# Half of q as a seventeenth pair of seven products, fourth block sums in place behind the last q part, and rates spread over six slots

## The chip, the cores and the metric

The kernel runs on one core of a Trainium2 chip. Its engines are TensorE (PE, with its weight loads shown as PEld), VectorE (DVE), ScalarE (ACT), GpSimd (POOL) and SyncE (SP, which issues nearly all DMAs). The metric is the device time of one execution in microseconds (us); several executions are taken and their median counts.

## The reference

One layer of a bidirectional hybrid encoder on x (1024 positions, 1024 channels, float32): an embedding LayerNorm; one input projection; two branches; a merge; an output projection; a last LayerNorm.

```python
h = layer_norm(x, emb_ln_g, emb_ln_b)
proj = h @ w_in                      # q k v z_a u z_b (512 each), g_a g_b (1024 each)
y_a = neighbourhood_attention(q, k, v, rpb) * silu(z_a)   # 8 heads x 64, q scaled by 1/8
u = centred_depthwise_conv(u, conv_w, conv_b)
y_b = (rg_lru(u, forward) + rg_lru(u, reverse)) * silu(z_b)
m = sigmoid(g_a + b0) * (y_a @ w_ba) + sigmoid(g_b + b1) * (y_b @ w_bb)
out = layer_norm(ALPHA * h + m @ w_out, ln_g, ln_b)
```

In `rg_lru`, log_a = -8 * softplus(-lambda) * r: softplus(-lambda), one number for each channel and direction, is what this text calls the rates.

## The kernel before

**Matrix products.** Every operand is split into a high and a low part of reduced width, and a product is three matmuls: high by high, low by high, high by low (`mm3`). TensorE reads 128x128 weights against 512 columns. The transposed input of the projection lies in four blocks of 512 x 512: B11, B12 (channels 0 to 511, positions 0 to 511 and 512 to 1023) and B21, B22 (channels 512 to 1023).

**Pairs of seven products.** Two blocks of 128 output columns of the input projection make a pair. A pair (`product`) is not computed as eight products of quarter size but as seven, in the manner of Strassen and Winograd: the left operands are the four weight quarters a11, a12, a21, a22 and their sums s1 = a21 + a22, s2 = s1 - a11, s3 = a11 - a21, s4 = a12 - s2; the right operands are B11, B21, B22 and the block sums T1 to T4. Each product is 12 matmuls, in the order a11, a12, s2, s1, s3, s4, a22 (`OPS`). Products s2, s3 and a22 go on into the PSUM bank of a11, s4 into that of s1 (`INTO`). Between them the bank is read out (`evacuate`): ScalarE copies it after a11 (u1) and after s2 (u2), and the bank of s1 after s1 (u3); VectorE then adds what each output block needs, and reads the bank of a11 once more after s3, ahead of a22.

**Slots.** Sixteen pairs make 112 slots, one for a product. In each slot the Python loop issues, in this order: the read-out of the product before, the high part of a weight of the next pair (`s_hi`), things hung into the slot with `at(slot, 0, ...)`, the product, the low part of a weight (`s_lo`), stores, one weight sum of the next pair (`s_sum`, slots 0 to 3) or the loads of the pair after that (`s_load`, slot 4), and things hung in with `at(slot, 1, ...)` (convolution, gates, scans of the second branch). The order of issue is written out by hand for all engines, and each engine works its queue in order.

**The stage before the pairs.** LayerNorm, transposes (`tile_in`), v (eight tiles, `v_part`, 24 matmuls each) and q. q has four blocks of 128 columns (m), each with two halves of 512 positions (n): eight parts (`q_part`) of 24 matmuls. ScalarE writes the high part of a q block (`q_hi`), VectorE the low part (`q_lo`), SP stores it to q_d (`q_store`), from where the attention loads it later. Between these, for the position tiles 4 to 7, the block sums are built: `t_full(i)` makes T1, T2 and T3, `t_last(i)` makes T4 with two VectorE subtractions and additions into a tile of its own, `t_hi` (ScalarE) and `t_lo` (GpSimd) split them. Parts (0, 0) and (1, 0) run within the v stage; the six others stand behind it. While they run, the weights of the first pair (u, columns 0 and 1) are loaded and split; those of the second are loaded behind the last q store. Then the rates follow in one piece, some 30 VectorE instructions of 8 columns with one Exp on ScalarE.

**Behind the pairs:** the attention with the second branch's projection as filler, the merge of the branches (`mb`), the output projection (`o`) with its LayerNorm.

Of the kernel before, what the change touches and what calls it, by code (L numbers as in the profile page):

```python
# [28 lines left out]
N_PAIR = 16  # L29
# [3 lines left out]
CONV_AT = (7, 24, 45, 66)  # L33
GATE_AT = (14, 24, 35, 45, 56, 66, 77, 87)
LATE_AT = (102, 102, 103, 104, 105)
HEAD_AT = 109
LO_POOL = ("a11", "a22")
HI_POOL = ("a12", "s2", "s1", "s3", "s4")
U_PAIRS = (0, 5)
# [28 lines left out]
def encoder_kernel(ctx, tc, x, gb1, gb, w_qk, w_v, w_s, w_ba, w_bb, w_gate, smalls, bias, w_out, out):  # L68
# [223 lines left out]
    def t_full(i):  # L292

        tt[i, 3] = wsp.tile([P, 4, P], F32, tag="a22", bufs=2, name=f"t3_{i}")[:]
        t12 = ln.tile([P, 2, 4, P], F32, tag="x", bufs=5, name=f"t12_{i}")
        tt[i, 1], tt[i, 2] = t12[:, 0], t12[:, 1]
        if i in (4, 6):
            tt["last"] = ln.tile([P, 2, 4, P], F32, tag="x", bufs=5, name=f"t4_{i}")
        tt[i, 4] = tt["last"][:, i % 2]
# [7 lines left out]
    def t_last(i):  # L307
        t4 = tt[i, 4]
        V.tensor_tensor(t4, f(B21[0], i), tt[i, 2], ALU.subtract)
        V.tensor_tensor(t4, t4, f(B21[1], i), ALU.add)  # L310
# [58 lines left out]
    def s_load(p, *names):  # L369
        for o in names if p < N_PAIR else ():  # L370
            t = wsp.tile([P, 4, P], F32, tag=o, bufs=2 if o == "a22" else 1, name=f"{o}_{p}f")
            SP.dma_start(t[:], w_s[p, ("a11", "a21", "a12", "a22").index(o)])
            s_a[p, o] = t

    def s_sum(p, *names):
        for o in names if p < N_PAIR else ():
            a, b, op = dict(s1=("a21", "a22", ALU.add), s2=("s1", "a11", ALU.subtract),
                            s3=("a11", "a21", ALU.subtract), s4=("a12", "s2", ALU.subtract))[o]
            t = s_a[p, o] = wsp.tile([P, 4, P], F32, tag=o, name=f"{o}_{p}f")
            V.tensor_tensor(t[:], s_a[p, a][:], s_a[p, b][:], op)  # L380
# [152 lines left out]
    qk_load(2)  # L533
# [10 lines left out]
    t_last(4)  # L544
    tile_in(5)
    q_hi(0, 0)
    t_hi(4, 2, 1, 3, 4)
    t_lo(4, 2, 1, 3, 4)
# [3 lines left out]
    keep(7)  # L552
    q_part(1, 0)
    t_full(5)
# [3 lines left out]
    t_last(5)  # L558
# [4 lines left out]
    t_hi(5, 2, 1, 3, 4)  # L563
    t_lo(5, 2, 1, 3, 4)
# [906 lines left out]
```

## Time and profile before

| | |
|---|---|
| three runs | 677.56, 678.9, 678.63 us; median 678.63 |
| profiled execution | 678.46 us, span 676.7 us, 9344 instructions |
| busy share of the span | PE 98%, PEld 82%, DVE 73%, ACT 54%, POOL 53% |
| granted TensorE clock, mean | 0.997 |
| chain that ended last | PE 89%, DVE 6%, DMA 2%, others about 1% or less |

The span runs from the first to the last instruction of the profiled execution; its own time is 1.8 us longer. In the rows of a timeline the first number is the start from the beginning of the span, the second the time that the instructions of the row took, and x the number of instructions; in brackets stands the idle time of that engine before the row and what ended it. A row of TensorE's waits has the total, the number of times and the longest, in us.

### The profile page before, as it was taken

The numbers are of one execution on the slowest core, as the hardware profiler recorded it, in microseconds if no ns is written. First come the engines' busy times: TensorE is split into PE (matmuls) and PEld (weight loads), VectorE is DVE, ScalarE is ACT, GpSimd is POOL, SyncE is SP. The second block draws the span as 40 slices with busy tenths as digits, with TensorE's granted clock in tenths as the row PEclk, the third lists the DMA queues.
The fourth block names the chain that finished last, engine by engine and source line by source line (L and its number), as shares of the span: only waits on it lengthen the run. The fifth ranks groups of instructions, "written<-read, shape, count | busy, mean of one in ns | idle before, by whom it ended". The sixth has DMA issues, their size and how long they took to land.

```text
span 676.7 us, 9344 instructions
## 1 busy us (share of the span) xinstructions
PE 665.2 (98%) x3201; PEld 555.7 (82%) x3201; DVE 492.7 (73%) x821; ACT 364.5 (54%) x612; POOL 355.8 (53%) x258
## 2 busy tenths in 40 slices
PE   8999999999999999999999999999999999999995
PEld 6888888888888887888788888888888878888884
DVE  6978747886998699879967785477787787443434
ACT  6554433256786676669576634477777554210110
POOL 6798632434677576567647444116155456334442
PEclk9999999999999999999999999999999999999998
DMA  8654353233434133431553456998793467412211
GB/s 326 244 179 170 122 206 126 77 110 123 125 128 144 40 103 115 170 126 48 195 178 122 173 191 254 316 366 296 255 323 132 162 220 281 178 62 94 93 63 62
DMA packets 48702, 113.39 MB, mean 168 GB/s; under 512 B 5056, under 2 KB 9744, under 8 KB 47120
## 3 DMA queue, kind: packets, MB, share of 16 engines
q1 hardware_dynamic: 48624, 112.81, 47.2%
q8 instruction: 25, 0.41, 0.3%
q14 instruction: 21, 0.17, 0.1%
q10 hardware_dynamic: 32, 0.01, 0.0%
HBM read 77.11 MB, written 35.68 MB: 167 GB/s over the span
## 4 chain that ended last, share of the span: by engine, by line
PE 89%; DVE 6%; DMA 2%; issue 1%; SPq 1%; ACT 0%; POOL 0%; DVEq 0%; POOLq 0%
PE a L134 30%; PE o L134 13%; PE mb L134 12%; PE s L134 11%; PE q L134 6%; PE v L328 6%; PE acc L1107 3%; PE s L1061 3%; PE pt L1083 3%; PE g L759 2%; DMA wqk_s<-in_w_qk_dram 2%; DVE ws_l L128 1%; PE tp L270 1%; DMA rsb<-rs_d 1%; DVE uc L717 1%
## 5 line engine op out<-in xcount | busy, mean ns | idle before, releaser
L134 PE MATMUL o<-wo_h,ml 128*128 128x512 f32 (+1 forms) x136 | 51.2, 377 | 0.0
L134 PE MATMUL o<-wo_l,mh 128*128 128x512 f32 (+1 forms) x136 | 51.2, 376 | 0.0
L134 PE MATMUL o<-wo_h,mh 128*128 128x512 f32 (+1 forms) x136 | 51.2, 376 | 0.0
L134 PE MATMUL a<-ht_h,ws_h 128*128 128x512 f32 x128 | 50.0, 390 | 0.0
L134 PE MATMUL a<-ht_l,ws_h 128*128 128x512 f32 x128 | 49.8, 389 | 0.0
L134 PE MATMUL a<-ht_h,ws_l 128*128 128x512 f32 x128 | 49.8, 389 | 0.0
L134 PE MATMUL a<-b_h,wa_h 128*128 128x512 f32 x128 | 49.8, 389 | 0.0
L134 PE MATMUL a<-b_h,wa_l 128*128 128x512 f32 x128 | 49.8, 389 | 0.0
L134 PE MATMUL a<-b_l,wa_h 128*128 128x512 f32 x128 | 49.8, 389 | 0.0
L1071 DVE CUSTOM_DVE_ANT_0 sc<-s,bias 128x384 f32<-128x384 f32 (+1 forms) x64 | 33.4, 522 | 21.6 <-PE s L1061 14.2
L1361 DVE SCALAR_TENSOR_TENSOR z<-z,o 128x512 f32<-128x512 f32 (+1 forms) x17 | 11.2, 656 | 51.0 <-PE o L134 51.0
L1091 ACT CAST pt_h<-pt 128x384 fp32r<-128x384 f32 x64 | 29.0, 453 | 25.3 <-PE pt L1083 17.3
L1371 POOL TENSOR_TENSOR z<-z,gb 128x1024 f32<-128x1024 f32 x7 | 16.8, 2400 | 48.5 <-ACT z L1370 48.5
L1076 ACT ACTIVATE p<-sc,summ 128x384 f32<-128x384 f32 (+1 forms) x64 | 37.8, 591 | 5.5 <-DVE summ L1071 5.3
L1340 ACT ACTIVATE sd<-mv,eps_z 128x1 f32<-128x1 f32 x8 | 2.4, 294 | 67.1 <-DVE mv L1366 67.1
L128 DVE TENSOR_TENSOR pt_l<-pt,pt_h 128x384 fp32r<-128x384 f32 x64 | 33.2, 519 | 2.1 <-ACT pt_h L1091 1.6
L328 PE MATMUL v<-wv,b_h 128*128 128x512 f32 x128 | 32.9, 398 | 0.6 <-ACT b_h L279 0.5
L867 POOL CAST wb_h<-wb 128x512 fp32r<-128x512 f32 x9 | 7.0, 779 | 47.4 <-DMA wb<-in_w_bb_dram 47.4
L1061 PE MATMUL s<-ks,qs 128*128 128x384 f32 (+1 forms) x128 | 31.4, 327 | 0.0
L1083 PEld LDWEIGHTS pt<-ident,p 128*128 128x128 f32 x176 | 23.1, 140 | 8.5
L1083 PE MATMUL pt<-ident,p 128*128 128x128 f32 x176 | 29.6, 272 | 0.0
L128 POOL TENSOR_TENSOR wb_l<-wb,wb_h 128x512 fp32r<-128x512 f32 x16 | 22.0, 1375 | 14.3 <-ACT wb_h L865 13.6
(438 smaller groups left out, 2204.2 us busy)
## 6 DMA issues: line engine op xcount, KB each, us to landing
ks<-k_d SPq DMA_DIRECT2D x8, 1024.0 KB, 7.5
h_d<-x SPq DMA_DIRECT2D x8, 512.0 KB, 5.0
v_d<-vs SPq DMA_DIRECT2D x8, 512.0 KB, 3.7
q_d<-q SPq DMA_DIRECT2D x8, 512.0 KB, 3.1
ga_d<-ga SPq DMA_DIRECT2D x16, 256.0 KB, 2.2
gb_d<-gb SPq DMA_DIRECT2D x16, 256.0 KB, 2.6
k_d<-k SPq DMA_DIRECT2D x8, 512.0 KB, 3.4
qs<-q_d SPq DMA_DIRECT2D x8, 512.0 KB, 5.5
```

Of the source, the lines that this page charges most:

```text
L128: eng.tensor_tensor(lo, full, hi.bitcast(F32), ALU.subtract)
L134: PE.matmul(o, a, b, start=first and i == 0, stop=last and i == len(prods) - 1, skip_group_check=not (first and last))
L328: PE.matmul(vos[i][:], a, wv[kind == "w"][k][:], start=vn[i] == 0, stop=vn[i] == 23)
L759: PE.matmul(o[:, n, :], w[:, 2 * d + b, :], us[b][:, n * HALF:(n + 1) * HALF], start=z == 0, stop=z == 1)
L1061: PE.matmul(o[:, :P * len(near(t))], q[:, t * P:(t + 1) * P], k[:, z, keys], start=z == 0, stop=z == 1)
L1071: V.tensor_tensor_reduce(s[:, :w], o[:, :w], heads[h][2][:, b0:b0 + w], -1.0, 3.0e38, ALU.add, ALU.min, accum_out=sums[h][0][:, t:t + 1])
L1076: A.activation(probs[h % 2][t][:], scs.pop((h, t))[:, :w], AF.Exp, bias=sums[h][0][:, t:t + 1], scale=-1.0, accum_out=sums[h][1][:, t:t + 1])
L1083: PE.transpose(tp[:, n * P:(n + 1) * P], probs[h % 2][t][:, z * P:(z + 1) * P], ident[:])
L1091: A.copy(pt[0][:, span(b)], tps[h, b][:, :P * len(near(b))])
L1107: PE.matmul(acc[g][:, d:d + w], vvs[h // 2][:, b, h % 2, :], pt[:, a:a + w], start=b in (1, 6) and z == 0, stop=z == 1 and b == (4, 7)[g])
L1361: V.scalar_tensor_tensor(z[:, cols], z[:, cols], ALPHA * TWICE, o, ALU.mult, ALU.add)
L1371: G.tensor_tensor(z[:], z[:], gb2[:, 0, :], ALU.mult)
```

## The change

- Blocks m = 2 and 3 of q leave the q parts and become the first pair: `N_PAIR` is 17, column 2 heads the list of pairs, and all slot numbers move by seven. `take_q` reads that pair out: add, scaled high part (ScalarE), low part and store (VectorE, SP).
- The pair's weights are loaded during the v stage into places that are free by then (the staging tile of the q weights, one of the x tiles); its sums are formed behind v of tile 6, its highs (all on ScalarE) and lows (all on VectorE) around q parts (0, 1) and (1, 1). The weights of the next pair are loaded one by one between those steps, its a22 last.
- T4 of the tiles 4 to 7 is formed in place of T2, once T2 has been split: all four `t_last` and their `t_hi` stand behind q part (1, 1) and ahead of that part's `q_hi`. `t_full` comes one step earlier in the tiles' order, and T3 takes four places instead of two.
- The rates are a generator, one piece in each of the slots 1 to 6.

```diff
@@ -26,17 +26,17 @@
 EPS = 1e-5
 TWICE = 4.0
 C_LRU = 8.0
-N_PAIR = 16
+N_PAIR = 17
 
 
 WARM = 18, 4, 6
-CONV_AT = (7, 24, 45, 66)
-GATE_AT = (14, 24, 35, 45, 56, 66, 77, 87)
-LATE_AT = (102, 102, 103, 104, 105)
-HEAD_AT = 109
+CONV_AT = (14, 31, 52, 73)
+GATE_AT = (21, 31, 42, 52, 63, 73, 84, 94)
+LATE_AT = (109, 109, 110, 111, 112)
+HEAD_AT = 116
 LO_POOL = ("a11", "a22")
 HI_POOL = ("a12", "s2", "s1", "s3", "s4")
-U_PAIRS = (0, 5)
+U_PAIRS = (1, 6)
 BLOCKS = (1, 0, 6, 2, 3, 4, 5, 7)
 SCORES = (0, 1, 2, 5, 6, 7, 3, 4)
 PV_LAG = 3
@@ -291,12 +291,10 @@
 
     def t_full(i):
 
-        tt[i, 3] = wsp.tile([P, 4, P], F32, tag="a22", bufs=2, name=f"t3_{i}")[:]
+        tag = ("a22", "a21", "a12", "a22")[i - 4]
+        tt[i, 3] = wsp.tile([P, 4, P], F32, tag=tag, bufs=2 if tag == "a22" else 1, name=f"t3_{i}")[:]
         t12 = ln.tile([P, 2, 4, P], F32, tag="x", bufs=5, name=f"t12_{i}")
         tt[i, 1], tt[i, 2] = t12[:, 0], t12[:, 1]
-        if i in (4, 6):
-            tt["last"] = ln.tile([P, 2, 4, P], F32, tag="x", bufs=5, name=f"t4_{i}")
-        tt[i, 4] = tt["last"][:, i % 2]
         t1, t2, t3 = (tt[i, c] for c in (1, 2, 3))
         A.copy(t3, tp4(i, 0))
         V.tensor_tensor(t1, tp4(i, 0), f(B11[0], i), ALU.subtract)
@@ -305,8 +303,8 @@
         V.tensor_tensor(t3, tp4(i, 1), t3, ALU.subtract)
 
     def t_last(i):
-        t4 = tt[i, 4]
-        V.tensor_tensor(t4, f(B21[0], i), tt[i, 2], ALU.subtract)
+        t4 = tt[i, 4] = tt[i, 2]
+        V.tensor_tensor(t4, f(B21[0], i), t4, ALU.subtract)
         V.tensor_tensor(t4, t4, f(B21[1], i), ALU.add)
 
     def t_hi(i, *cs):
@@ -367,27 +365,33 @@
     s_a, s_w = {}, {}
 
     def s_load(p, *names):
-        for o in names if p < N_PAIR else ():
-            t = wsp.tile([P, 4, P], F32, tag=o, bufs=2 if o == "a22" else 1, name=f"{o}_{p}f")
-            SP.dma_start(t[:], w_s[p, ("a11", "a21", "a12", "a22").index(o)])
+        for z, o in enumerate(names if p < N_PAIR else ()):
+            if p:
+                t = wsp.tile([P, 4, P], F32, tag=o, bufs=2 if o == "a22" else 1, name=f"{o}_{p}f")[:]
+            else:
+                if z == 0:
+                    place = dict(pool=ln, tag="x", bufs=5) if o == "a21" else dict(pool=wpl, tag="ws", bufs=1)
+                    both = place.pop("pool").tile([P, 2, 4, P], F32, name=f"{o}_{p}f", **place)
+                t = both[:, z]
+            SP.dma_start(t, w_s[p, ("a11", "a21", "a12", "a22").index(o)])
             s_a[p, o] = t
 
     def s_sum(p, *names):
         for o in names if p < N_PAIR else ():
             a, b, op = dict(s1=("a21", "a22", ALU.add), s2=("s1", "a11", ALU.subtract),
                             s3=("a11", "a21", ALU.subtract), s4=("a12", "s2", ALU.subtract))[o]
-            t = s_a[p, o] = wsp.tile([P, 4, P], F32, tag=o, name=f"{o}_{p}f")
-            V.tensor_tensor(t[:], s_a[p, a][:], s_a[p, b][:], op)
+            t = s_a[p, o] = wsp.tile([P, 4, P], F32, tag=o, name=f"{o}_{p}f")[:]
+            V.tensor_tensor(t, s_a[p, a], s_a[p, b], op)
 
     def s_hi(p, o):
         if p < N_PAIR:
             s_w[p, o] = pair(wsp, [P, 4, P], f"w{o}_{p}", tag="w" + o)
-            (G.tensor_copy if p and o in HI_POOL else A.copy)(s_w[p, o][0][:], s_a[p, o][:])
+            (G.tensor_copy if p and o in HI_POOL else A.copy)(s_w[p, o][0][:], s_a[p, o])
 
     def s_lo(p, o):
         if p < N_PAIR:
             hi, lo = s_w[p, o]
-            lo_of(G if o in LO_POOL else V, lo[:], s_a[p, o][:], hi[:])
+            lo_of(G if p and o in LO_POOL else V, lo[:], s_a[p, o], hi[:])
 
 
     K0, K1, KS, BOTH = range(4), range(4, 8), range(8), range(2)
@@ -530,7 +534,6 @@
 ...
     keep(5)
-    qk_load(2)
 ...
@@ -541,76 +544,81 @@
     v_store(3)
     keep(6)
     q_part(0, 0, slice(256, HALF))
-    t_last(4)
     tile_in(5)
     q_hi(0, 0)
-    t_hi(4, 2, 1, 3, 4)
-    t_lo(4, 2, 1, 3, 4)
+    t_hi(4, 2, 1, 3)
+    t_lo(4, 2, 1, 3)
     tile_lo(5)
     q_lo(0, 0)
     q_store(0, 0)
     keep(7)
+    t_full(5)
     q_part(1, 0)
-    t_full(5)
     q_hi(1, 0)
     q_lo(1, 0)
     q_store(1, 0)
-    t_last(5)
+    t_hi(5, 2, 1, 3)
+    t_lo(5, 2, 1, 3)
     for kind in "hwa":
         v_part(4, kind, KS)
     tile_in(6)
     v_hi(4)
-    t_hi(5, 2, 1, 3, 4)
-    t_lo(5, 2, 1, 3, 4)
     tile_lo(6)
     v_lo(4)
     v_store(4)
     t_full(6)
+    t_hi(6, 2, 1, 3)
+    t_lo(6, 2, 1, 3)
     for kind in "hwa":
         v_part(5, kind, KS)
+    s_load(0, "a11", "a12")
     tile_in(7)
     v_hi(5)
-    t_hi(6, 2, 1, 3)
-    t_lo(6, 2, 1, 3)
     tile_lo(7)
     v_lo(5)
     v_store(5)
-    t_last(6)
-    t_hi(6, 4)
-    t_lo(6, 4)
     t_full(7)
+    t_hi(7, 2, 1, 3)
+    t_lo(7, 2, 1, 3)
+    s_load(0, "a21", "a22")
+    s_load(1, "a21")
     for kind in "hwa":
         v_part(6, kind, KS)
     v_hi(6)
-    t_last(7)
     v_lo(6)
     v_store(6)
+    s_load(1, "a12")
+    s_sum(0, "s1", "s2", "s3", "s4")
     for kind in "hwa":
         v_part(7, kind, KS)
     v_hi(7)
     v_lo(7)
     v_store(7)
-    s_load(0, "a11")
-    for m in range(4):
-        for n in BOTH if m > 1 else (1,):
-            q_part(m, n)
-            if m < 2:
-                qk_prep(m + 2)
-                if m == 0:
-                    qk_load(3)
-                    t_hi(7, 2, 1, 3, 4)
-                    t_lo(7, 2, 1, 3, 4)
-                    s_load(0, "a21", "a22", "a12")
-                else:
-                    s_sum(0, "s1", "s2", "s3", "s4")
-            q_hi(m, n)
-            q_lo(m, n)
-            q_store(m, n)
-            if m > 1:
-                for w in (OPS[:2], OPS[2:4], OPS[4:6], OPS[6:])[2 * (m - 2) + n]:
-                    s_hi(0, w)
-                    s_lo(0, w)
-    s_load(1, "a11", "a21", "a12", "a22")
+    s_load(1, "a11")
+    for o in OPS[:3]:
+        s_hi(0, o)
+        s_lo(0, o)
+    q_part(0, 1)
+    for o in OPS[3:5]:
+        s_hi(0, o)
+        s_lo(0, o)
+    q_hi(0, 1)
+    q_lo(0, 1)
+    q_store(0, 1)
+    q_part(1, 1)
+    for o in OPS[5:]:
+        s_hi(0, o)
+        s_lo(0, o)
+    for i in range(4, NT):
+        t_last(i)
+    for i in range(4, NT):
+        t_hi(i, 4)
+    q_hi(1, 1)
+    q_lo(1, 1)
+    q_store(1, 1)
+    for i in range(4, NT):
+        t_lo(i, 4)
+    s_load(1, "a22")
     for pl in (ln, wpl, hb12, pst, ps0):
         pl.release()
     psd = tc.alloc_tile_pool(name="psd", bufs=1, space=bass.MemoryType.PSUM, reuse_waits="tile")
@@ -623,23 +631,30 @@
-    V.tensor_scalar(smh[:], sm[:], 0.5, None, ALU.mult)
...
-    V.tensor_scalar(nsp[:], t0[:], -C_LRU, None, ALU.mult)
+    def decay_rates():
+        V.tensor_scalar(smh[:], sm[:], 0.5, None, ALU.mult)
+        V.tensor_scalar(t0[:], lam, -1.0, None, ALU.mult)
+        V.tensor_tensor(t0[:], lam, t0[:], ALU.min)
+        A.activation(t0[:], t0[:], AF.Exp)
+        yield
...
+        for n in (17, 15, 13, 11, 9, 7, 5, 3, 1):
+            V.tensor_tensor(t2[:], t2[:], t1[:], ALU.mult)
+            V.tensor_scalar(t2[:], t2[:], 1.0 / n, None, ALU.add)
+            if n in (13, 7, 1):
+                yield
...
+        V.tensor_scalar(nsp[:], t0[:], -C_LRU, None, ALU.mult)
+        yield
@@ -676,6 +691,23 @@
                     V.scalar_tensor_tensor(z[:], z[:], 1.0, c[:], ALU.add, ALU.mult)
                 SP.dma_start(dst[m0 + mi][:, n * HALF:(n + 1) * HALF], z[:])
             return [squash, store]
+        return consume
+
+    def take_q():
+
+        def consume(mi, n, add, o, c=None):
+            c = o if c is None else c
+            if add is not None:
+                V.tensor_tensor(c[:], add[:], o[:], ALU.add)
+            t = lru.tile([P, 2, HALF], F32R, tag=("us0", "r", "i", "us1")[2 * mi + n], name=f"q2{mi}{n}")
+
+            def high():
+                A.activation(t[:, 0, :], c[:], AF.Copy, scale=0.125)
+
+            def store():
+                V.scalar_tensor_tensor(t[:, 1, :], c[:], 0.125, t[:, 0, :].bitcast(F32), ALU.mult, ALU.subtract)
+                SP.dma_start(q_d[2 + mi][:, :, halves[n]], t[:].bitcast(F32))
+            return [high, store]
         return consume
 
     def take_k(m0):
@@ -901,9 +933,12 @@
     def gates_b(j):
         return lambda: take_zg(gb_d, 2 * j, "gb", SM_BM + 8)
 
-    takes = [lambda: take_u(0), lambda: take_zg(zb_d, 0, "zb"), lambda: take_zg(za_d, 0, "za"), gates_a(0), gates_a(1),
+    takes = [take_q, lambda: take_u(0), lambda: take_zg(zb_d, 0, "zb"), lambda: take_zg(za_d, 0, "za"), gates_a(0), gates_a(1),
              lambda: take_u(2), gates_b(0), lambda: take_zg(zb_d, 2, "zb"), gates_a(2), gates_b(1),
              lambda: take_k(0), gates_a(3), lambda: take_k(2), lambda: take_zg(za_d, 2, "za"), gates_b(2), gates_b(3)]
+    rates = decay_rates()
+    for slot in range(1, 7):
+        at(slot, 1, lambda: next(rates))
     for t, slot in enumerate(CONV_AT):
         conv_stage(t, slot)
     for n, slot in enumerate(GATE_AT):
@@ -1416,7 +1451,7 @@
     wt = w_in.reshape(NK, P, 40, P).transpose(2, 1, 0, 3)
     branch = [w[0].reshape(4, P, NK, P).transpose(2, 1, 0, 3) for w in (g["w_branch_attn"], g["w_branch_lru"])]
 
-    heads = [16, 20, 12, 24, 26, 18, 32, 22, 28, 34, 4, 30, 6, 14, 36, 38]
+    heads = [2, 16, 20, 12, 24, 26, 18, 32, 22, 28, 34, 4, 30, 6, 14, 36, 38]
     w_s = np.stack([np.stack([wt[m + c][:, 4 * kk:4 * kk + 4] for kk in range(2) for c in range(2)]) for m in heads])
 
     gw = g["lru_gate_w"][0].transpose(0, 2, 3, 1, 4).reshape(2, 4, 2, 64, 2, 64)
```

More of the change, by code (lines that the diff above doesn't have):

```diff
@@ L625, in encoder_kernel @@
     lam = sm[:, SM_LAM:SM_LAM + 8]
[L626 to L642 removed]
+    def decay_rates():
[4 more added lines that the diff above has]
+        yield
+        V.tensor_scalar(t1[:], t0[:], 2.0, None, ALU.add)
+        V.reciprocal(t1[:], t1[:])
+        V.tensor_tensor(t0[:], t0[:], t1[:], ALU.mult)
+        V.tensor_tensor(t1[:], t0[:], t0[:], ALU.mult)
+        V.tensor_scalar(t2[:], t1[:], 1.0 / 21.0, 1.0 / 19.0, ALU.mult, ALU.add)
+        yield
[4 more added lines that the diff above has]
+                yield
+        V.tensor_tensor(t2[:], t2[:], t0[:], ALU.mult)
+        V.tensor_scalar(t0[:], lam, -1.0, 0.0, ALU.mult, ALU.max)
+        V.scalar_tensor_tensor(t0[:], t2[:], 2.0, t0[:], ALU.mult, ALU.add)
+        V.tensor_scalar(sp[:], t0[:], C_LRU, None, ALU.mult)
+        V.tensor_scalar(nsp[:], t0[:], -C_LRU, None, ALU.mult)
+        yield
     ups, ucs, hsum = {}, {}, {}
```

15 lines of the change are left out of this document (removed).

## The prediction

> **What bounds the kernel now.** I read the engine shares first, then the chain of work that ended last, then TensorE's own waits, then the stages by windows.
>
> ```profile
> span 676.7 us, 9344 instructions
> PE 665.2 (98%) x3201; PEld 555.7 (82%) x3201; DVE 492.7 (73%) x821; ACT 364.5 (54%) x612; POOL 355.8 (53%) x258
> ...
> 72.93 32.64 PE q L134 x144
> 105.57 8.16 PE a L134 x36
> 113.73 2.72 PE s L134 x12
> 116.45 2.72 PE a L134 x12
> ...
> 581.37 87.36 PE o L134 x408
> ```
>
> TensorE is busy for 98% of the span, and the chain is TensorE from the q stage to the last output product. The row at 72.93 is the six q parts: 144 matmuls in 32.64 us, 0.2267 us each, 5.44 us for a part of 24. The rows from 105.57 are the seven products of the first pair, 12 matmuls and 2.72 us each. (The page's 389 ns for such a matmul is its own length; neighbours overlap.)
>
> ```profile
> PE a L134 <- DVE w L792: 0.4, 1, 0.4
> ...
> 72.90:105.60 32.70, 32.70 (x146) 27.09 (x145) 15.99 (x23) 12.25 (x21) 13.16 (x9) 1.00 0.48 163
> 105.60:124.60 19.00, 19.00 (x85) 15.73 (x84) 16.41 (x48) 4.88 (x8) 6.50 (x7) 1.00 0.48 153
> ```
>
> TensorE's longest wait at such a product is 0.4 us, once in the whole span (columns: total, times, longest). By windows (length, then busy time of PE, PEld, DVE, ACT and POOL, granted clock, DMA share, GB/s) TensorE fills both stages at a clock of 1.00. So TensorE's instruction count sets the time, as long as nobody makes it wait. Every microsecond of a new wait is added to the end, since nothing behind it has slack to give back.
>
> **The change, part by part.** *Matmuls.* Four q parts go (m = 2 and 3, both halves: 96 matmuls), seven products come (84). Twelve fewer at 0.2267 us: **-2.72 us**. The pair starts behind q part (1, 1) at 72.93 + 2 x 5.44 = 83.81, 21.76 us earlier than the first pair before. Without a wait its products would start at: a11 83.81, a12 86.53, s2 89.25, s1 91.97, s3 94.69, s4 97.41, a22 100.13. The two loads of q weights give way to four pair loads of the same bytes, so traffic stays as it is.
>
> *The conditions of three products.* Products s2, s3 and a22 add into the bank of a11. Product s2 may start only when ScalarE has copied a11 out (u1), s3 when it has copied the sum with s2 (u2), a22 when VectorE has added u3 to that bank. Each engine works in order, so the question is what stands ahead of u1, u2 and that add. That is the issue order of the changed code:
> - ScalarE: the highs of s4 and a22, four highs of T4 (`t_hi(i, 4)`), the high of q (1, 1), u1, one weight, the table load and Exp of the rates, u2.
> - VectorE: lows of s4 and a22, eight in-place sums (`t_last`), the low of q (1, 1), the sums s1 and s2 of pair 1, three rate steps, then the add for a12.
> - SP: the store of q (1, 1), and only behind it the load of a22 of pair 1, which the sum s1 of pair 1 reads.
>
> So u2 waits for Exp, Exp for the rate steps, these for a weight sum of the *next* pair, this for a load, and the load stands behind a store that waits for the in-place sums.
>
> *When the in-place sums end.*
>
> ```profile
> 61.08 1.45 DVE L309 TENSOR_TENSOR t<-b_h,t 128x512 f32<-128x512 f32 x1
> 62.56 1.67 DVE L310 TENSOR_TENSOR t<-t,b_l 128x512 f32<-128x512 f32 x1
> ...
> 77.54 0.68 DVE L309 TENSOR_TENSOR t<-b_h,t 128x512 f32<-128x512 f32 x1
> 78.26 0.69 DVE L310 TENSOR_TENSOR t<-t,b_l 128x512 f32<-128x512 f32 x1
> ...
> 60.70 5.94 POOL L128 TENSOR_TENSOR ht_l<-t,ht_h 128x512 fp32r<-128x512 f32 x4 [2.27 <-ACT ht_h L314]
> ...
> 79.37 2.17 ACT L314 CAST ht_h<-t 128x512 fp32r<-128x512 f32 x4
> ...
> 101.40 1.28 DVE L128 TENSOR_TENSOR ws_l<-s_0f,ws_h 128x512 fp32r<-128x512 f32 x2
> 105.60 0.60 ACT L355 ACTIVATE q<-q 128x512 fp32r<-128x512 f32 x1 [3.82 <-PE q L134]
> ...
> 106.23 0.69 DVE L360 SCALAR_TENSOR_TENSOR q<-q,q 128x512 fp32r<-128x512 f32 x1 [3.55 <-ACT q L355]
> ```
>
> Part (0, 1) ends on TensorE at 78.37. Its ScalarE copy (0.60) and VectorE low (0.69) follow, then two more lows (1.28 the pair), so the sums begin near 81.2. I take VectorE to be free by then: it has no `t_last` in the v stage any more, about 3 us a tile by the first two rows. Undisturbed, a tile's two sums come at 0.72 and 0.61, so eight cost 5.3 us with GpSimd idle (end 86.5), and 12.5 us if all run as the two rows at 61.08 do, beside GpSimd (end 93.7). Here GpSimd's low of a tile (5.94 / 4 = 1.5 us) starts only after ScalarE's copy (0.6) of that tile, so the first sum of the next tile is free and the second one opposed: 1.35 + 3 x (0.69 + 1.67) = 8.4, end **89.6**. I take that value, as the sums alternate with those lows.
>
> *From there to s3.*
>
> ```profile
> 106.73 1.28 ACT L629 ACT_TABLE_LOAD   x1
> 108.44 0.21 ACT L629 ACTIVATE sp<-sp 128x8 f32<-128x8 f32 x1 [0.42 <-DVE sp L628]
> 108.55 0.57 ACT L939 COPY u<-a 128x512 f32<-128x512 f32 x1
> ...
> 106.84 1.28 DVE L626 TENSOR_SCALAR smh<-sm 128x60 f32<-128x60 f32 x1
> 108.04 0.16 DVE L627 TENSOR_SCALAR sp<-sm 128x8 f32<-128x8 f32 x1
> 108.23 0.17 DVE L628 TENSOR_TENSOR sp<-sm,sp 128x8 f32<-128x8 f32 x1
> ...
> 115.53 0.69 DVE L380 TENSOR_TENSOR s_1f<-a_1f 128x512 f32<-128x512 f32 x1
> 116.25 0.69 DVE L380 TENSOR_TENSOR s_1f<-s_1f,a_1f 128x512 f32<-128x512 f32 x1
> ...
> 107.96 2.05 SPq L372 DMA_DIRECT2D a_1f<-in_w_s_dram  x4
> ...
> a_0f<-in_w_s_dram SPq DMA_DIRECT2D x4, 256.0 KB, 5.3
> a_1f<-in_w_s_dram SPq DMA_DIRECT2D x4, 256.0 KB, 3.9
> q_d<-q SPq DMA_DIRECT2D x8, 512.0 KB, 3.1
> ```
>
> The last T4 high ends 0.6 later (90.2), the high of q (1, 1) at 90.7, u1 at 91.2. Product s2 was due at 89.25: it waits 2.0 us. The low of q (1, 1) ends at 91.4, its store takes SP 0.5 (2.05 / 4), and the load behind it lands 3.9 after its issue (the first pair of before, also behind a q store; 5.3 for the crowded a_0f, 3.1 for a q store as the short end): 95.8. Sums s1 and s2 of pair 1: 1.4 (97.2). Three rate steps took 1.56 in before, beside GpSimd (106.84 to 108.40); undisturbed I put the first at 0.3 and so all at 0.6; I take 1.0, as GpSimd wakes on the same sum s2 (98.2). In before the table load ran ahead of its Exp's wait (106.73 against 108.40). As built now, the wait stands in front of the load: 1.28 + 0.21, then u2 with 0.57: **100.3**. Product s3 was due at 94.69, and starts **5.6 us late**, the 2.0 at s2 among it.
>
> *a22.*
>
> ```profile
> 109.73 0.17 DVE L636 TENSOR_TENSOR sp<-sp,sp 128x8 f32<-128x8 f32 x1
> 109.93 0.17 DVE L637 TENSOR_SCALAR sp<-sp 128x8 f32<-128x8 f32 x1
> ...
> 120.79 0.68 DVE L658 TENSOR_TENSOR up<-u,a 128x512 f32<-128x512 f32 x1
> ```
>
> A rate step comes every 0.20 us. Between Exp (99.7) and the add for a22, VectorE has 17 such steps (3.4) and four operations of 512 at 0.6 to 0.7 (2.6), then the add (0.7): 106.4. TensorE has run s3 and s4 by 105.7, so a22 waits **0.7 us**. (Before, the add of 120.79 ended 0.4 us ahead of its product.)
>
> *What costs nothing.* Pair 1 begins at 109.2; its first weights are split by then, and what is left of the rates and q's lows is done within its first two products. The store of each q block replaces a store of the same size. The gates and convolutions move seven slots, as the pairs do. TensorE's own work up to 72.93 stays as it is; VectorE is relieved there. If that cover fails, the first sums of pair 0 come late, and the in-place sums with them, one for one.
>
> **The sum.** -2.72 + 5.6 + 0.7 = +3.6 us. The profiled execution took 678.46 us (span 676.7 and 1.8 around it), 0.17 under the median of the three runs: 678.46 + 3.6 = **682.0 us**.
>
> [...]
>
> ```profile
> 157.04 1.28 ACT L772 ACT_TABLE_LOAD   x1
> 158.33 1.15 ACT L772 ACTIVATE a<-r,nsp 128x1024 f32<-128x1024 f32 x1
> ```
>
> Here an operation follows a table load 0.01 us after its end. [...]
>
> **Rivals.**
> 1. *All covered* (faster). The chain from the last in-place sum to the end of u2 is 10.7 us long; with 94.69 as the due time the sums would have to end at 84.0, 2.8 us after they begin, where unopposed they need 5.3. It takes a landing under 1.5 us besides, or sums that start far earlier than the copy of q (0, 1) lets them. Then only the matmuls count: 675.7. Chance 0.08.
> 2. *A short chain* (no change). Sums unopposed (86.5), landing 3.1, rate steps 0.6: u2 ends at 96.0, a wait of 1.3 and 0.7, 2.0 in all: 677.7; with the landing of 3.9, 678.5. For it: the second row pair. Against: GpSimd is woken by these very sums. Chance 0.18.
> 3. *A long chain.* The landing of the crowded load (5.3, so 1.4 more) gives 683.4, all eight sums opposed (end 93.7, so 4.1 more) 686.1, both 687.5. For it: the rows at 61.08 and 62.56. Against: GpSimd has four lows here, not a stream. Chance 0.08.
> 4. *The clock.* TensorE stands still for 2.0 and then 3.6 us. If its clock falls with that, and a product of 12 matmuls runs at half pace, 2.72 us come on top: 684.7. No window of before shows such a gap or a clock under 1.00 here. [...] Chance 0.04, and 0.02 for the drain above.
>
> That the change does not do what it says is out: as built, TensorE has twelve matmuls less.
>
> **How the numbers follow.** My forecast of 682.0 has the other 0.60; its own range, with the sums ending between 88 and 91 and landings of 3.1 to 4.5, is 679.6 to 684.2. A measurement of this kernel can tell about 0.2%, 1.4 us. Faster than that: rival 1 and the shortest of rival 2, 0.10. Within: the rest of rival 2, 0.16. Slower: 0.74. The range takes in rival 2 from its shorter form and stops short of the long chain with both prices: 677.7 to 685.0.
>
> **What would show it.** Right: TensorE waits at s2 for u1 (about 2 us), at s3 for u2 (about 3.6), at a22 for the add (about 0.7), nowhere else; ScalarE idle ahead of its table load; VectorE idle ahead of the sum s1 of pair 1 for the load. Wrong: no idle time of TensorE between the q parts and pair 1 (rival 1), in-place sums at 0.7 each (rival 2), or waits in later pairs, which I have put at nothing.

## The result, and the profile after

| | before | after |
|---|---|---|
| median of six runs each, same chip | 678.51 us (677.56 to 679.34) | 683.41 us (682.51 to 683.9) |
| ratio, 95% interval | | 1.0071, 1.0058 to 1.0084 |
| profiled execution, its span | 678.46, 676.7 us | 683.23, 681.5 us |

The change makes the kernel 0.7% slower, with twelve matmuls less. The page of the kernel after, its shares of busy time:

```profile
span 681.5 us, 9354 instructions
PE 664.7 (98%) x3189; PEld 553.7 (81%) x3189; DVE 498.3 (73%) x835; ACT 364.7 (54%) x615; POOL 351.9 (52%) x261
```

TensorE's busy time has hardly gone down (665.2 before), its idle time is up by 5.3 us. TensorE's waits in the kernel after (total, times, longest; of these three, only the wait for `w` stood in the kernel before):

```profile
PE a L134 <- ACT u L978: 3.5, 1, 3.5
...
PE a L134 <- ACT u L974: 0.8, 1, 0.8
...
PE a L134 <- DVE w L824: 0.3, 1, 0.3
```

L974 is u1 and L978 is u2: product s2 waits 0.8 us, product s3 3.5. The chain of work that ended last leaves TensorE behind q part (0, 1) and comes back to it only at s3, through the steps that the prediction lists, in their order (start, length):

```profile
73.89 2.23 PE q L134 x10
...
81.94 0.61 DVE t L307
...
84.60 1.71 DVE t L307
86.33 1.67 DVE t L308
...
88.64 0.70 DVE t L308
...
89.89 0.60 ACT q L353
...
90.51 0.70 DVE q L358
...
91.23 0.51 SPq L362
...
91.84 4.12 DMA a_1f<-in_w_s_dram
...
95.98 0.70 DVE s_1f L384
...
96.71 0.69 DVE s_1f L384
97.40 0.10 DVE smh L636
...
98.24 1.28 ACT L639
...
99.65 0.58 ACT u L978
...
100.27 4.61 PE a L134 x12
104.88 2.74 PE s L134 x12
...
107.62 10.88 PE a L134 x48
```

In-place sums (81.94 to 89.34), high and low of q (1, 1), store, load, two sums of pair 1, rates, table load and Exp, u2, s3. The timelines show the idle time that the prediction named as its signs: VectorE stands still for the load, ScalarE for the rates, ahead of its table load.

```profile
95.98 0.69 DVE L384 TENSOR_TENSOR s_1f<-a_1f 128x512 f32<-128x512 f32 x1 [4.78 <-DMA a_1f<-in_w_s_dram]
```
```profile
98.24 1.28 ACT L639 ACT_TABLE_LOAD   x1 [6.77 <-DVE sp L638]
99.53 0.21 ACT L639 ACTIVATE sp<-sp 128x8 f32<-128x8 f32 x1
```

The row of the chain at 100.27 shows something more: twelve matmuls take 4.61 us, not 2.72. The timeline of TensorE there, and the windows (granted clock third from the right):

```profile
84.61 0.39 PE L134 MATMUL a<-b_h,wa_h 128*128 128x512 f32 x1
...
100.72 0.63 PE L134 MATMUL a<-ht_h,ws_l 128*128 128x512 f32 x1
101.14 0.63 PE L134 MATMUL a<-ht_l,ws_h 128*128 128x512 f32 x1
...
103.28 0.63 PE L134 MATMUL a<-ht_h,ws_l 128*128 128x512 f32 x1
103.70 0.48 PE L134 MATMUL a<-ht_l,ws_h 128*128 128x512 f32 x1
104.02 0.40 PE L134 MATMUL a<-ht_h,ws_h 128*128 128x512 f32 x1
```
```profile
101.00:102.00 1.00, 1.00 (x4) 0.71 (x4) 1.00 (x3) 0.19 (x1) 0.00 (x0) 0.50 0.00 0
104.00:105.00 1.00, 1.00 (x6) 0.81 (x5) 0.87 (x5) 0.00 (x0) 0.06 (x1) 1.00 0.00 0
```

The first row is the start of the pair. Eight matmuls of s3 come 0.427 us apart at a clock of 0.50; from 104.02 on they are 0.23 apart again.

**Where the time went.** The last row of the chain holds four products, a22 first, so pair 1 begins at 107.62 + 2.72 = 110.34: 36.45 us after q part (0, 1) at 73.89. Before, the six q parts took 32.64 up to the same products (72.93 to 105.57). So this stage lost 3.81 us: -2.72 for the matmuls, +1.1 around s2 (the wait of 0.8, and first matmuls 0.33 and 0.24 us apart behind it), +3.7 at s3, +1.7 for the half clock. In the first pairs behind it nothing waits anew, but from the first gate matmul to the first score matmul TensorE needs 285.9 us (151.0 to 436.9) instead of 285.4 (146.2 to 431.6). Together 4.3 us. The profile after also starts this stage 1.0 us later (73.89 against 72.93), so that its first score matmul comes 5.3 us later; 0.5 of that comes back behind it, and the spans differ by 4.8. The medians differ by 4.9 (3.9 to 5.7 by the interval of the ratio), and 4.3 lies within; the start varies from run to run by about as much as it differs here (last experiments).

### The profile page after: what moved, and what is told of

Its sections match the earlier page's. It is cut to its first block, busy times and chain, and to the rows that moved or that the text cites. A ratio compares the mean times of both kernels' runs of the same rounds, so it can differ in the third digit from the quotient of the medians.

```text
span 681.5 us, 9354 instructions
## 1 busy us (share of the span) xinstructions
PE 664.7 (98%) x3189; PEld 553.7 (81%) x3189; DVE 498.3 (73%) x835; ACT 364.7 (54%) x615; POOL 351.9 (52%) x261
## 4 chain that ended last, share of the span: by engine, by line
PE 88%; DVE 7%; DMA 2%; issue 1%; ACT 1%; SPq 1%; DVEq 0%; ACTq 0%
PE a L134 30%; PE mb L134 13%; PE o L134 13%; PE s L134 12%; PE v L326 6%; PE acc L1142 4%; PE s L1096 3%; PE pt L1118 3%; PE q L134 2%; PE g L791 2%; DMA wqk_s<-in_w_qk_dram 2%; DVE ws_l L128 1%; PE tp L270 1%; DVE wa_l L128 1%; DMA a_1f<-in_w_s_dram 1%
## 5 line engine op out<-in xcount | busy, mean ns | idle before, releaser
L134 PE MATMUL a<-ht_h,ws_h 128*128 128x512 f32 x136 | 54.0, 397 | 4.3 <-ACT u L978 3.5
L134 PE MATMUL a<-ht_h,ws_l 128*128 128x512 f32 x136 | 53.7, 395 | 0.0
L134 PE MATMUL a<-ht_l,ws_h 128*128 128x512 f32 x136 | 53.5, 393 | 0.0
L134 PE MATMUL a<-b_h,wa_l 128*128 128x512 f32 x136 | 53.0, 389 | 0.0
L134 PE MATMUL a<-b_h,wa_h 128*128 128x512 f32 x136 | 52.9, 389 | 0.0
L134 PE MATMUL a<-b_l,wa_h 128*128 128x512 f32 x136 | 52.9, 389 | 0.0
L134 PEld LDWEIGHTS a<-ht_h,ws_h 128*128 128x128 f32 x136 | 25.9, 190 | 11.1 <-ACT u L978 3.9
L128 POOL TENSOR_TENSOR ht_l<-t,ht_h 128x512 fp32r<-128x512 f32 x16 | 22.5, 1434 | 15.8 <-ACT ht_h L312 15.8
L134 PEld LDWEIGHTS a<-ht_l,ws_h 128*128 128x128 f32 x136 | 26.0, 191 | 5.6
```

The source lines that it names most:

```text
L128: eng.tensor_tensor(lo, full, hi.bitcast(F32), ALU.subtract)
L134: PE.matmul(o, a, b, start=first and i == 0, stop=last and i == len(prods) - 1, skip_group_check=not (first and last))
```

## The experiments

All medians stand beside runs of the kernel before on the same chip at the same time.

**One link of the chain taken out: the load, or the rates.** The first kernel loads a22 of pair 1 ahead of the q stores, the second moves the rates to slots 8 to 13.

```diff
-    s_load(1, "a22")            # behind the T4 lows
     s_load(1, "a11")
+    s_load(1, "a22")
```
```diff
-    for slot in range(1, 7):
+    for slot in range(8, 14):
         at(slot, 1, lambda: next(rates))
```

> One load moves: a22 of pair 1 is issued right behind a11 of pair 1 (behind the store of v of tile 7) and no longer behind the store of q (1, 1). Theory (the chain: u2 behind Exp, Exp behind the rate steps, these behind the sum s1 of pair 1, this behind that load): VectorE goes from the low of q (1, 1) straight into s1, u2 ends some 4.7 us earlier, near 95.6 on the changed kernel's own scale, where s3 is due at 96.4; the 3.5 us wait at s3 and the slow clock behind it (1.9 us) both go, the 0.8 us at s2 stays: about 678.0 us, 5.4 less than the changed kernel. Rival (VectorE and ScalarE are simply too full there, the load only happens to be what the trace names): the wait moves on to the rate steps and the add for a22, at least half of the 3.5 us stays, 680.5 us or more.

> The six pieces of the rates go into slots 8 to 13 instead of 1 to 6; loads and block sums stay as in the change. Theory (chain): another link is cut. VectorE still stands until the load lands near 96, but ScalarE has no Exp ahead of u2, so s3 starts on time; the add for a22 is then the next, and comes within 0.5 us of its due time: 678.0 to 678.5 us, s2's 0.8 us still there, no slow clock. Rival (the late load itself stalls TensorE, with or without Exp): 2 us or more of the wait stays, at a22 or in pair 1: 680.5 us or more.

| | median | before | ratio, 95% interval |
|---|---|---|---|
| load early | 678.51 us (678.07 to 680.04) | 678.57 | 1.0001, 0.9993 to 1.0009 |
| rates late | 677.8 us (676.21 to 678.14) | 678.57 | 0.9986, 0.9977 to 0.9994 |

The timeline of TensorE with the early load, rows with a wait:

```profile
91.30 0.50 PE L134 MATMUL a<-ht_h,ws_h 128*128 128x512 f32 x1 [0.80 <-ACT u L974]
...
97.62 0.50 PE L134 MATMUL a<-ht_h,ws_h 128*128 128x512 f32 x1 [0.54 <-ACT u L978]
```

And ScalarE with the late rates:

```profile
90.13 0.58 ACT L974 COPY u<-a 128x512 f32<-128x512 f32 x1
...
93.82 0.59 ACT L978 COPY u<-a 128x512 f32<-128x512 f32 x1 [2.58 <-PE a L134]
```

Either cut gives back 4.9 to 5.6 us, all that the change had cost, though each leaves the other half of the chain as it was. Both times are near what was expected. With the early load s3 waits 0.54; with the late rates u2 follows 2.58 us of idle ScalarE, when TensorE is done with s2, and s3 doesn't wait at all; the one new wait there is 0.33 at a22 for the add. In neither profile does the clock fall ahead of the end of the kernel (672.3 and 671.2). So s3 was late because Exp stood in ScalarE's queue ahead of u2 *and* its rate steps stood in VectorE's queue behind a sum that needed the late load. The wait of 0.80 at s2 stays in both: it is u1 behind the T4 highs, another chain.

**The in-place sums in the v stage.** Tiles 4 to 6 are done there, as before the change; only tile 7 stays behind q part (1, 1).

```diff
+    t_last(4)                    # behind t_lo(5, 2, 1, 3)
+    t_last(5); t_hi(4, 4); t_lo(4, 4)      # around the T1 to T3 of tile 6
+    t_last(6); t_hi(5, 4); t_lo(5, 4)      # around those of tile 7
+    t_hi(6, 4); t_lo(6, 4)       # behind v_hi(6)
-    for i in range(4, NT):
-        t_last(i)                # behind q part (1, 1); the highs and lows likewise
+    t_last(7); t_hi(7, 4); t_lo(7, 4)
```

> The in-place sums of tiles 4, 5 and 6 go back into the v stage (behind the split of tile 5, behind the block sums of tiles 6 and 7), their highs and lows with them; only tile 7 stays behind q part (1, 1). Loads and rates as in the change. Theory (chain, which begins at the in-place sums): the high of q (1, 1) runs as soon as its product ends, u1 is on time, and store, load, sums and Exp all come some 5 us earlier; u2 ends near 95.0 where s3 is due at 95.65. No wait at s2 and s3, at most 0.3 us at a22, no slow clock: 676.0 us, or 677.0 if the start of the kernel stays 1 us later as in the profile of the change. Rival (the q stage has too little VectorE time for a whole pair's weights): the sums s1 to s4 and the lows of pair 0 come later by the 3 to 5 us that the in-place sums take in the v stage, and products of pair 0 wait: 679 us or more.

Measured: 680.55 us (679.88 to 681.87), ratio 1.003, 1.0019 to 1.004. The expectation missed by some 4 us; the time is that of the rival. The timelines of TensorE (its rows with a wait) and of VectorE:

```profile
85.08 0.50 PE L134 MATMUL a<-b_h,wa_h 128*128 128x512 f32 x1 [0.94 <-DVE q L358]
...
98.66 0.50 PE L134 MATMUL a<-ht_h,ws_h 128*128 128x512 f32 x1 [2.39 <-ACT u L984]
```
```profile
77.33 1.78 DVE L384 TENSOR_TENSOR s_0f<-a_0f 128x512 f32<-128x512 f32 x1
79.03 1.78 DVE L384 TENSOR_TENSOR s_0f<-a_0f,s_0f 128x512 f32<-128x512 f32 x1
...
84.35 0.68 DVE L358 SCALAR_TENSOR_TENSOR q<-q,q 128x512 fp32r<-128x512 f32 x1
...
86.15 0.68 DVE L307 TENSOR_TENSOR t<-b_h,t 128x512 f32<-128x512 f32 x1
...
88.74 0.69 DVE L358 SCALAR_TENSOR_TENSOR q<-q,q 128x512 fp32r<-128x512 f32 x1 [1.18 <-ACT q L353]
```

The three tiles' sums push pair 0's own weight sums to a time when GpSimd works beside them (1.78 us for each of the two rows at 77.33 and 79.03, with GpSimd busy without a break from 72 to 80.26; 0.68 for each of the two at 74.33 and 74.94 in the kernel after, with GpSimd idle). With them everything behind on VectorE is late: the low of q (0, 1) at 84.35, for which a11 now waits, the sums of tile 7 at 86.15, the low of q (1, 1) at 88.74, only 1.8 us earlier than in the kernel after. The store, the load and the rates follow as they did, and s3 still waits 2.39: with the late load in place, relieving the start of the chain is not enough. I had cleared the queue ahead of the chain and not seen that the same queue fills again from the front.

**Both: load early and sums in the v stage.**

> The moves of the first and the third of these runs together: the load of a22 of pair 1 early, and the in-place sums of tiles 4 to 6 in the v stage. Theory (chain): u2 has some 4 us to spare, the add for a22 as well; TensorE has no new wait at all and keeps the whole 2.72 us of the twelve matmuls: 675.8 us (676.8 with the later start). Rival (VectorE too full): 678 us or more.

Measured: 677.09 us (676.36 to 677.9), ratio 0.9974, 0.9965 to 0.9984: faster than before, though not by the whole 2.72. s2, s3 and a22 don't wait, as the theory had it; a11 does, against it, 0.93 us for the low of q (0, 1).

**That low first.**

```diff
-    for o in OPS[:3]:
+    for o in OPS[:2]:
         s_hi(0, o); s_lo(0, o)
     q_part(0, 1)
-    for o in OPS[3:5]:
-        s_hi(0, o); s_lo(0, o)
     q_hi(0, 1); q_lo(0, 1); q_store(0, 1)
+    for o in OPS[2:5]:
+        s_hi(0, o); s_lo(0, o)
```

> The version with both the early load of a22 of pair 1 and the block sums of tiles 4 to 6 in the v stage, with one more move: the high and low parts and the store of the q part (0,1) go ahead of the high and low parts of pair 0's s2, s1 and s3 weights on ScalarE and VectorE. In that version product a11 of pair 0 waited 0.93 us for the low of the q part, which frees its PSUM bank and was queued on VectorE behind four low parts. Theory: without three of them ahead (3 x 0.6 us) the low ends near 83.0, before a11 is due at 84.3; the 0.93 us go, no other wait of TensorE comes, and the time is 677.09 - 0.93 = 676.2 us, 2.4 us below the kernel before, of which 2.72 us would be the 12 matmuls saved. Rival (the low parts of s2, s1 and s3 are late then, or the high of q holds up ScalarE for them): a wait of 0.5 us or more at s2, s1 or s3 takes its place and the time stays at 677.0 or above.

Measured: 676.67 us (676.09 to 678.99), ratio 0.9972, 0.9961 to 0.9982. The low now ends at 83.2 and a11 doesn't wait; the only new row is a wait of 0.34 at a22 for VectorE's add, which the theory did not have. That is 2.3 us below the runs of before beside it, close to the 2.4 expected, and s2, s1 and s3 don't wait as the rival said. What it leaves of the 2.72 led to the gate matmuls.

**The gate matmuls.**

```diff
-            t = lru.tile([P, 2, HALF], F32R, tag=("us0", "r", "i", "us1")[2 * mi + n], ...)
+            t = lru.tile([P, 2, HALF], F32R, tag=("a", "r", "i", "wh")[2 * mi + n], bufs=(1, 1, 1, 2)[2 * mi + n], ...)
```

> The fastest version so far with one change of names: the four q tiles of the new pair take the buffers of a, r, i and wh of the gate stages instead of those of us0, r, i and us1, so that the two us tiles are placed later and at another address. In the kernel before, the 16 groups of gate matmuls (us as the moving operand) ran at 389 ns a matmul, and a group and the product behind it took 3.62 us; in all changed kernels 394 ns and 3.67 us, some 0.6 us in all with the places where it differs. Theory (the address of us, moved by the tags that the q tiles take, makes these matmuls slower): 389 ns again and 676.67 - 0.6 = 676.1 us. Rival (it is the length of the program or something else about the gate stages): 394 ns still and 676.7 us.

Measured: 675.94 us (675.85 to 676.97), ratio 0.9958, 0.9946 to 0.997: the fastest version, 0.4% below the kernel before. The gate matmuls of the kernel after and of this one (shortest, median and longest in ns, first and last start):

```profile
L791 PE MATMUL g<-us,gw_h x32: 394/394/394, 151.0 to 371.1; 128*128 128x512 f32 x32
```
```profile
L797 PE MATMUL g<-us,gw_h x32: 389/389/389, 144.9 to 364.6; 128*128 128x512 f32 x32
```

389 ns is what they took before the change, and from the first of them to the first score matmul it is 285.4 us again (144.9 to 430.3). This edit of the q tiles' tags alone did it; that it is the address of `us` is argued, as the tags move other tiles of that pool too.

**The half clock.** Extra matmuls behind product s1, which wait for nothing, fill part of TensorE's gap ahead of s3.

```diff
+        if (p, o) == (0, "s3"):
+            fill = psd.tile([P, 2, HALF], F32, tag="gates", name="fill")
+            for _ in range(8):      # 4, 8 or 15
+                PE.matmul(fill[:, 0, :], B11[0][:, 0, :P], B11[0][:, 0, :], start=True, stop=True)
```

> The changed kernel with one addition: eight extra 128x512 matmuls (high part of pair 0's a11 weights by the high part of one input block, into a PSUM bank that nobody uses before slot 21; their output is read by nobody) are issued behind product s1 of pair 0, ahead of product s3. They wait for nothing and need 8 x 0.227 = 1.8 us of the 3.5 us in which TensorE waits for u2, so the gap without a matmul shrinks to 1.7 us; u2 and all else stay where they are. Theory (the idle gap itself lowers the granted clock, and the lower clock costs product s3 1.89 us): s3 begins at the same time as in the changed kernel, 3.5 us late, but takes 2.72 instead of 4.61 us, and the kernel takes 683.4 - 1.9 = 681.5 us. Rival (s3 is slow because of something that runs beside it, the DMA traffic or the other engines' use of PSUM, or the clock drops whatever TensorE does): s3 still takes about 4.6 us and the time stays at 683.4, or 1.8 us above if the extra matmuls delay s3.

Measured: 684.36 us (683.67 to 684.54), ratio 1.0077, 1.0065 to 1.0089. This first form took pair 0's a11 weights as its operand, and so held their buffer: ScalarE's cast of pair 1's weights into it moved from 90.84 to 98.81, right ahead of the table load, and s3 began 1.2 us later, behind a gap of 2.75 us. The kernel tested a new wait as much as the clock. Still the half clock came, from 102.76 to 106.17, 1.3 us after TensorE had started again.

> The changed kernel with eight extra 128x512 matmuls behind product s1 of pair 0, as in the first filler run, but both operands now come from an input block (B11) that no other engine writes any more. In the first filler run they read pair 0's a11 weights, whose buffer ScalarE was to overwrite with pair 1's: its cast moved from 90.8 to 98.8, directly ahead of the table load, and u2 came 1.2 us later. Without that, u2 ends near 100.2 as in the changed kernel, the extra matmuls end near 98.6, and 1.7 us without a matmul are left. Theory (the long gap lowers the granted clock for some 3.4 us, in both runs so far: after 3.5 us and after 2.75 us, not after 2.4): s3 runs at full clock, 2.72 instead of 4.4 us, and the time is 683.4 - 1.7 = 681.7 us. Rival (the clock falls for another reason at this place): s3 or s4 has matmuls at a pitch of 0.43 us again and the time is 683.4 or above.

> The changed kernel with four such extra matmuls on the input block: the gap without a matmul is 3.5 - 0.9 = 2.6 us, between the 2.4 us without a lower clock and the 2.75 us with one. If the length of the gap decides with a bound near 2.5 us, s3 or s4 shows a pitch of 0.43 us; if what counts is a stretch of fixed places, either can come.

> The changed kernel with fifteen extra matmuls on the input block behind product s1: 15 x 0.227 = 3.4 us, so that next to nothing of the 3.5 us without a matmul is left ahead of s3. With four and with eight of them the profiled run still had some 3.4 us at half clock behind the gap (3.0 and 1.8 us long), though the eight brought the median from 683.4 to 681.55 with single runs from 679.8 to 683.7. Theory (idle time of TensorE, whatever its length, can bring the half clock, and no idle time cannot): no matmul at a pitch of 0.43 us, s3 takes 2.72 us from its start near 100.3, the time is 683.4 - 1.7 = 681.7 us and its runs lie within 1.5 us of each other. Rival (these extra matmuls do not count as work for the clock, or it falls for another reason): some 8 matmuls of s3 or s4 at 0.43 us again, and 683.4 us.

| extra matmuls | gap before s3 | half clock | median |
|---|---|---|---|
| none | 3.5 us | 100.5 to 103.9 | 683.41 us, ratio 1.0071, 1.0058 to 1.0084 |
| 4 | 3.05 us | 100.9 to 104.4 | 683.26 us (one run) |
| 8 | 1.79 us | 100.9 to 104.3 | 681.55 us (679.78 to 683.7), ratio 1.004, 1.0025 to 1.0055 |
| 15 | none | none | 682.57 us (680.83 to 684.43), ratio 1.0055, 1.004 to 1.0069 |

The gap and the half clock are those of the profiled run. The runs with four and eight were made on another chip than the first filler kernel, those with fifteen on a third, each with the kernel before beside them. TensorE with eight and with fifteen extra matmuls:

```profile
100.45 0.50 PE L134 MATMUL a<-ht_h,ws_h 128*128 128x512 f32 x1 [1.79 <-ACT u L978]
100.79 0.51 PE L134 MATMUL a<-ht_h,ws_l 128*128 128x512 f32 x1
101.09 0.63 PE L134 MATMUL a<-ht_l,ws_h 128*128 128x512 f32 x1
```
```profile
96.62 3.56 PE L997 MATMUL fill<-b_h 128*128 128x512 f32 x15
100.15 0.50 PE L134 MATMUL a<-ht_h,ws_h 128*128 128x512 f32 x1
100.49 0.40 PE L134 MATMUL a<-ht_h,ws_l 128*128 128x512 f32 x1
100.73 0.40 PE L134 MATMUL a<-ht_l,ws_h 128*128 128x512 f32 x1
```

With fifteen, the profile has no idle time and no half clock, with s3 starting at the same place: the rival falls there, and with what follows the idle time is the cause. My sharper form of it, that a gap must be longer than about 2.4 us, fell too: 1.79 us brought the half clock in this profile, 2.39 us in the sums-in-the-v-stage kernel did not.

The mean clock of each run shows that a short gap does it in some executions only. It is 0.995 to 0.998 in the runs of the kernel before and of the versions whose waits here stay below 1 us (not 1, as it also falls at the end of the kernel: at 672.52 in the first profile of before, 3.8 us after the last matmul). With eight extra matmuls, two of seven runs have 0.994 (683.68, the profiled one, and 683.7 us), the others 0.996 or 0.997 (679.78 to 682.06). In the sums-in-the-v-stage kernel three of eight have 0.993 or 0.994 (680.79 to 681.87), while its profiled run has 0.997 (679.88). With fifteen, one run of six has 0.993 (684.43); no trace shows where its clock fell, and the spread of 3.6 us misses the 1.5 that was expected.

What decides can be estimated from the windows of the profiles (0.02 us long for the kernel after, 1 us for the others). In the kernel after the clock fell at 100.463, rose at 103.876 and fell at 677.315, when TensorE had finished: 3.413 us apart, then 573.44, which is 168 times that. The three filler kernels with a half clock have the same two distances within 0.02 us, from 102.76, 100.94 and 100.92 on. So in these four profiles the changes lie as on a grid of 3.413 us, which lies elsewhere in each.

| profile | gap | fall | idle time in the grid step that ends there |
|---|---|---|---|
| kernel after | 96.77 to 100.27 | 100.46 | 3.2 us |
| first filler | 98.72 to 101.47 | 102.76 | 2.1 us |
| 4 extra matmuls | 97.59 to 100.64 | 100.94 | 3.05 us |
| 8 extra matmuls | 98.66 to 100.45 | 100.92 | 1.79 us |
| sums in the v stage | 96.27 to 98.66 | none | 0.8 and 1.6 us |

In the last row the grid is counted back 169 steps from the fall at the end (673.96), the only one of that profile: a step ends at 97.10 and cuts the gap in two. The first filler kernel gives one more case: its last matmul ends at 674.58, a step ends at 676.20 with 1.6 us of idle time in it, and the clock falls only one step later, at 679.61. So in these traces the clock falls for the next step when TensorE stood still for more than some 1.6 to 1.8 us of a step, about half, and where the grid lies against a gap is luck. This is an estimate from the few stretches named; no run was made to test it.

Against the runs of before beside them (678.99 and 678.66), eight matmuls brought 2.3 us and fifteen 1.0 where 1.7 was expected. With fifteen, the profile had the 1.4 us at the first score (435.5 against 436.9) and lost them again at 545 to a 0.66 us wait for ScalarE and others near it, where in the kernel before the chain runs through two DMAs (1.58 and 4.22 us); whether that belongs to the extra matmuls was not tried.

**The start.** In all changed kernels the second group of the v stage began later than in the first profile of before (16.95; 17.98 in the kernel after).

> The kernel before with only its weight input lengthened from 16 to 17 pairs, as in the changed kernel: the added first pair lies in DRAM and is never read, each pair is read from one place further on. Instructions and their order are those of the kernel before. Theory (the changed kernels start 0.4 to 1.3 us later, by the second group of the v stage, because their inputs lie elsewhere in DRAM and the loads of x and of the v weights are issued and land later): that group begins 0.4 to 1.3 us later than in the kernel before (16.95 in its profile), and the time is 678.9 to 679.8 us. Rival (the later start comes with the changed program or is chance): 678.5 us within 0.2, and the group begins near 16.95.

> The kernel before once more, for a second profile of it. If the start is fixed by the program, the second group of the v stage begins at 16.95 and the q part (0,1) at 72.93, as in its first profile, within 0.1; if it varies from run to run, it is off by up to the 0.9 us by which the five changed kernels differ among themselves (17.34 to 18.23).

Measured: 678.59 us (677.84 to 679.27) with the longer input, ratio 0.9995, 0.9987 to 1.0004, group at 17.45; 679.17 us for the kernel before again, group at 17.69. The chain of that second profile:

```profile
74.00 32.64 PE q L134 x144
```

The longer input alone has its group 0.5 us later, as its theory had it, but its time is that of the rival, and the unchanged kernel moves by more: its six q parts take 32.64 as in the first profile, but begin at 74.00 instead of 72.93. So the start varies by a microsecond between two runs of one program, and the start of the kernel after (73.89) lies within that: it need not be a cost of the change, and the first profile of before was an early one.

## Why the prediction was right, and where it was not

The forecast was 682.0 us against 683.41, slower by 3.4 where 4.9 was measured. Its chain of waits is the measured one, link for link; the half clock behind them was only a rival.

- *Matmuls, -2.72.* Right. With nearly all the waits gone, the fastest version is 3.05 us below the runs of before beside it; the interval of its ratio makes that 2.0 to 3.7.
- *In-place sums, 8.4 us long, end 89.6.* They took 7.4 (81.94 to 89.34). Not one sum in each of three tiles was opposed by GpSimd, as I had put it, but both sums of one tile (1.71 and 1.67 from 84.60 on, beside GpSimd's two lows from 84.00 to 87.45); the others ran at 0.6 to 0.7 a sum. As the pair began 0.8 us later than forecast, the end came out right by chance.
- *s2, 2.0 us.* 0.8, or 1.1 with the slower matmuls behind it; u1 came 1.0 us earlier, counted from the pair's start, for the same reason.
- *From the store to u2.* Store 0.51 (0.5), landing 4.12 (3.9), sums 1.4 (1.4), rates 0.84 (1.0), table load and Exp 1.28 and 0.2, u2 ended at 100.23 (100.3). The drain, to which the prediction gave a chance of 0.02, is shown by no run: Exp begins 0.01 us after the load's end (98.24 + 1.28, then 99.53).
- *s3 5.6 us late, s2's share in it.* 4.8, counted from the pair's own start (100.27 against 84.61 + 10.88). The difference is again the sums.
- *a22, 0.7.* No wait. VectorE's add (in the first timeline below) ended at 106.38, as forecast (106.4), but the slow clock brought the product to 107.62: a term that I had left out covers it. Without the slow clock it is smaller too: with fifteen extra matmuls the add ended at 105.86 and a22 began at 105.92, 0.15 late (the second, with rows of TensorE).

```profile
105.69 0.69 DVE L701 TENSOR_TENSOR c<-u,a 128x512 f32<-128x512 f32 x1
```
```profile
105.17 0.69 DVE L701 TENSOR_TENSOR c<-u,a 128x512 f32<-128x512 f32 x1
...
105.54 0.39 PE L134 MATMUL s<-b_l,ws_h 128*128 128x512 f32 x1
105.92 0.50 PE L134 MATMUL a<-ht_h,wa_h 128*128 128x512 f32 x1
```

- *The clock, rival 4 at 0.04.* It came: eight matmuls at half pace (0.427 us apart at a clock of 0.50), 1.7 us, not the twelve of the rival. This is the term that was mis-sized: its chance was not small, as by the estimate above, on a grid of 3.413 us, a forecast gap of 3.6 us has at least 1.8 us in one step wherever the grid lies; all six runs of the kernel after have a mean clock of 0.991 to 0.995. Waits overstated by 1.5 and the clock left out at 1.7 nearly cancel by luck, and so the stage's loss of 3.81 stands so close to the 3.6 of the sum.
- *What costs nothing.* Pair 1 begins without a wait, as put. The gate matmuls cost 0.5 that no step of the prediction had.
- *Rivals 1 to 3.* The waits are there, the landing was the middle one, and neither all sums nor none were opposed.

## What to carry to other kernels

Follow each release of a shared accumulator through its engine's queue: one operation that needed a late load, placed ahead of an evacuation, held up TensorE here for 3.5 us while VectorE stood 4.78 us for the load. Here cutting one of the two links behind the store was enough, the early load or the late rates; relieving the start of the chain was not. The queue that was cleared at one place filled at another: work moved onto a VectorE that was already late shifted its neighbours into GpSimd's time, where two sums took 1.78 us each for 0.68. And price a TensorE gap like those here, 1.79 to 3.5 us, with the half clock behind it: 1.7 us in the kernel after, and with eight extra matmuls in two runs of seven, by their mean clock of 0.994.

## What the runs showed of the hardware

- In the four profiles with a half clock, TensorE's clock changed on a grid of 3.413 us, which lay elsewhere in each. It fell to 0.50 for one step after idle times of 1.79, 2.75, 3.05 and 3.5 us, in one case only 1.3 us after work had begun again; a gap of 2.39, which the grid cut into 0.8 and 1.6, did not bring it down in the profile (mean clock 0.997), though it seems to have in three other runs of eight (0.993 or 0.994).
- The same 128x512 matmul, same operands by name, ran at 394 ns in the kernel after and at 389 with other tags for the q tiles of its pool: 0.5 us in this kernel.
- In the kernel after, VectorE's sums of two 128x512 tiles took 0.68 us at 81.86 and 83.19, with GpSimd idle, and 1.78 and 1.67 at 84.52 and 86.33, beside its lows. Not each one beside GpSimd was longer: that at 71.99 took 0.72.
- Two profiles of one kernel differed by 1.07 us in when the same row starts (72.93 and 74.00); a landmark late in the span has to be compared by differences inside the span.
